# Half of the third branch's merge products issued inside the convolution stage of a hybrid Hyena, FNet, mLSTM and mixture-of-experts layer

## The chip, the cores and the metric

The kernel runs on one core of a Trainium2 chip. The metric is device microseconds of one execution on that core; lower is better. A profiled execution shows what the engines did: PE (TensorE, the matrix engine), DVE (VectorE), ACT (ScalarE), POOL (GpSimd) and SP (SyncE, which here only starts transfers). Each engine takes its instructions in order.

## The reference, cut to what matters

One layer over 1024 tokens of width 1024, all in float32. Three branches (a Hyena long convolution, a grouped FNet and a bidirectional mLSTM) each give 512 channels. The merge projects each branch to 1024 channels, weighs it by a sigmoid gate and sums:

```python
def merge_branches(y_hy, y_fn, y_ml, gate_pre, lp):
    B, L, _ = gate_pre.shape
    dt = gate_pre.dtype
    ys = jnp.stack([y_hy, y_fn, y_ml], axis=2).astype(dt)
    proj = jnp.einsum("blkc,kcd->blkd", ys, lp["w_branch"])
    g = jax.nn.sigmoid(gate_pre.astype(jnp.float32)).reshape(B, L, N_BRANCH, D_MODEL).astype(dt)
    return jnp.sum(g * proj, axis=2) @ lp["w_out"]
```

The change is in the product `ys[2] @ w_branch[2]`, the mLSTM branch `y_ml`. Nothing that is computed changes.

## The kernel before, in words

A float32 product is made of three products of a shorter type. `split` (L215, L216) writes a value's upper part (ACT, a cast) and the rest (DVE or POOL, a subtraction); `mm3` (L230 to L232) issues upper by upper, lower by upper and upper by lower into one PSUM tile. So every operand that comes from DRAM costs a transfer, a cast on ACT and a subtraction on DVE or POOL, and every product three instructions on PE.

The kernel's stages follow one another: filters, projections, mLSTM, FNet, the gate projections, the Hyena convolutions (`stage_conv`), the merge (`stage_merge`), the output projection and the experts. The mLSTM and the FNet results lie in DRAM (`yd[2]`, `yd[1]`) long before the convolutions begin. The Hyena result `yd[0]` is written when they end.

**The convolutions.** Four passes (order 0 and 1, each for two halves of 256 channels), each of eight blocks `(par, fb)`: four of the even part, four of the odd part. A block has a forward product (`conv_fwd`, tiles `gp`: 12 instructions of 256 columns for an even block, 24 for an odd one). DVE then multiplies with the filter (`kk`, L1057), sums (`t`, L1059) and splits into `yh` (ACT) and `yl` (DVE). The inverse product (`conv_inv`, tiles `acc`, 12 instructions of 256 or 512 columns) follows two blocks later. At the fifth block the next pass's input is prepared (`conv_in`): DVE folds the previous pass's output (`f`), PE transposes it (L1023, 16 instructions a pass), ACT copies it (`raw`), DVE and ACT split it (`u2`, `u1`). That input is the result of `conv_out`, a chain on DVE over the second half of the pass before. In PSUM `gp` has two banks and `acc` six, all eight.

**The merge.** A loop over the branches 2, 1, 0 and, in each, over eight blocks `d` of 128 output channels. Per `d` PE issues 24 instructions of 512 columns (two halves of the tokens, four channel tiles `k`, three products). The weights `m` come from DRAM (256 KB; cast on ACT, subtracted on POOL) and so does the gate `g` (512 KB). For the first branch DVE writes `acc = (g + 1) * p` (L1539); for the other two it multiplies in `g`, and POOL adds. The branch's four input tiles `y` (512 KB each) go through the buffers `y` of pool `GA`, two in all, so the load of the third waits until the first is split (L216 `yl`). Gates have three buffers, raw weights two, output weights `w` in pool `GT` two. During the second branch the eight tiles of `w_out` are loaded too.

**Order.** Tile's scheduler orders each engine's instructions by its own estimate of time; the program's order and the priorities are only its input. SP starts nearly all transfers, in one queue, and a transfer that waits for a buffer holds back those behind it.

## Time and profile before

| | us |
|---|---|
| runs: lowest, median, highest of 3 | 1661.92, 1670.61, 1671.79 |
| the profiled execution's own time | 1670.78 |
| its span, first to last instruction | 1669.0 |
| convolutions, from the first forward product | about 906 to 1078 |
| first branch of the merge | about 1078 to 1123 |
| second and third branch | about 1123 to 1208 |

Positions are microseconds from the start of the span. A row of the view by stretches gives the busy time of each engine in it and the number of its instructions, the clock granted to TensorE as a share of 2.4 GHz (0.5 is the lower level, 1.2 GHz), the share of the 16 DMA engines' time in use, and GB/s. A matrix instruction's own duration is longer than its place in the queue, since the next starts before it ends: what one costs is read from start to start.

### The profile page before, as it was taken

The page shows a single profiled execution, that of the slowest core. Times are in us where ns is not written, and L with a number is a line of the kernel's source. Part 1 is how long each engine was busy: PE and PEld are TensorE (multiplying, and loading weights), DVE is VectorE, ACT ScalarE, POOL GpSimd, SP SyncE. Part 2 cuts the span into 40 slices and gives each one's busy share as a digit, 9 for nine tenths or more (in the row PEclk, how much of TensorE's full clock was granted, in tenths as well). Part 3 has the DMA queues.
Part 4 walks back from the last instruction along what each step waited for, and adds up shares of the span by engine and source line. Part 5 has one row for each costly group of instructions (what it writes and reads, how often), then busy time and mean ns, then how long its engine had stood idle before and what let it go on. Part 6 is the DMA issues. An engine that isn't in the chain of part 4 may idle for free. (4 is left out here: it accounts for less than half of the span.)

```text
span 1669.0 us, 22629 instructions
## 1 busy us (share of the span) xinstructions
PE 1557.4 (93%) x8489; PEld 1307.7 (78%) x8489; DVE 1179.0 (71%) x1764; ACT 686.2 (41%) x1052; POOL 303.1 (18%) x277
## 2 busy tenths in 40 slices
PE   6999999999999999899988899999999869999992
PEld 2678877788888887778877788888888769999992
DVE  3898785966786869788644999953255567767776
ACT  3566454433222124444424443332033444544553
POOL 0000000000000001000002000127523353565641
PEclk8999999999999999999998998999999979999996
DMA  7453576422232374877424433685363388999984
GB/s 287 139 199 137 213 239 219 144 81 81 101 110 89 129 261 169 295 265 245 157 107 159 140 102 100 229 313 180 135 255 114 139 252 251 300 282 289 264 233 169
DMA packets 125570, 315.97 MB, mean 189 GB/s; under 512 B 17689, under 2 KB 43281, under 8 KB 125458
## 3 DMA queue, kind: packets, MB, share of 16 engines
q1 hardware_dynamic: 113354, 279.77, 48.6%
q0 software_dynamic: 10496, 32.36, 8.1%
q10 hardware_dynamic: 1608, 2.37, 0.4%
q8 instruction: 68, 1.11, 0.3%
q14 instruction: 44, 0.36, 0.1%
HBM read 227.53 MB, written 86.91 MB: 188 GB/s over the span
## 5 line engine op out<-in xcount | busy, mean ns | idle before, releaser
L230 PE MATMUL gp<-ht,wh 128*128 128x512 f32 x768 | 303.9, 396 | 4.6 <-ACT wh L215 3.5
L232 PE MATMUL gp<-ht,wl 128*128 128x512 f32 x768 | 302.1, 393 | 0.9 <-DVE wl L216 0.9
L231 PE MATMUL gp<-ht,wh 128*128 128x512 f32 x768 | 302.5, 394 | 0.0
L230 PEld LDWEIGHTS gp<-ht,wh 128*128 128x128 f32 x768 | 145.0, 189 | 37.7 <-ACT wh L215 4.4
L232 PEld LDWEIGHTS gp<-ht,wl 128*128 128x128 f32 x768 | 145.0, 189 | 31.1 <-DVE wl L216 1.5
L231 PEld LDWEIGHTS gp<-ht,wh 128*128 128x128 f32 x768 | 145.1, 189 | 29.0 <-issue 0.2
L230 PE MATMUL pb<-xh,gh 128*128 128x224 f32 x512 | 142.7, 279 | 0.0
L231 PE MATMUL pb<-xl,gh 128*128 128x224 f32 x512 | 141.6, 277 | 0.8 <-issue 0.8
L232 PE MATMUL pb<-xh,gl 128*128 128x224 f32 x512 | 141.7, 277 | 0.0
L801 DVE SCALAR_TENSOR_TENSOR u<-z,hy_cw,u 128x945 f32<-128x945 f32 (+2 forms) x96 | 117.3, 1222 | 13.3 <-ACT u L793 11.1
L216 DVE TENSOR_TENSOR wl<-w,wh 128x1024 fp32r<-128x1024 f32 x57 | 70.4, 1236 | 58.5 <-ACT wh L215 58.1
L215 ACT CAST wh<-w 128x1024 fp32r<-128x1024 f32 x57 | 59.8, 1051 | 122.1 <-PE gp L231 83.4
L232 PEld LDWEIGHTS pb<-xh,gl 128*128 128x128 f32 x512 | 99.4, 194 | 0.8 <-issue 0.8
L230 PEld LDWEIGHTS pb<-xh,gh 128*128 128x128 f32 x512 | 99.3, 194 | 0.3 <-ACT xh L215 0.2
L231 PEld LDWEIGHTS pb<-xl,gh 128*128 128x128 f32 x512 | 99.4, 194 | 0.1
L801 DVE SCALAR_TENSOR_TENSOR u<-z,ml_cw,u 128x945 f32<-128x945 f32 (+2 forms) x64 | 77.9, 1220 | 27.4 <-ACT u L793 26.4
L786 ACT ACTIVATE z<-gp,b_cols 128x512 f32<-128x512 f32 x46 | 31.4, 684 | 136.8 <-PE gp L232 136.8
L216 POOL TENSOR_TENSOR ml<-m,mh 128x512 fp32r<-128x512 f32 x24 | 35.2, 1468 | 208.8 <-ACT mh L215 208.8
L949 POOL MEMSET z<- 128x1024 f32 x1 | 1.0, 961 | 359.1 <-DVE u L801 359.1
L786 ACT ACTIVATE z<-gp,bh 128x512 f32<-128x512 f32 x46 | 31.4, 684 | 76.4 <-PE gp L232 56.6
L1806 DVE TENSOR_TENSOR gl<-x,gh 128x1024 fp32r<-128x1024 f32 x33 | 40.5, 1233 | 29.1 <-ACT gh L1804 21.6
L1778 POOL DMA_INDIRECT sum<-y,sidx x26 | 45.4, 1744 | 79.5 <-DVE y L1887 75.9
(618 smaller groups left out, 3986.9 us busy)
## 6 DMA issues: line engine op xcount, KB each, us to landing
w<-in_ada_rest SPq DMA_DIRECT2D x32, 512.0 KB
w<-in_w_gu SPq DMA_DIRECT2D x32, 512.0 KB
x<-in_w_gu SPq DMA_DIRECT2D x32, 512.0 KB
w<-in_w_gate SPq DMA_DIRECT2D x24, 512.0 KB
g<-gd SPq DMA_DIRECT2D x24, 512.0 KB
gd<-z SPq DMA_DIRECT2D x23, 512.0 KB
r<-in_ada_in SPq DMA_DIRECT2D x16, 512.0 KB
pd<-ft SPq DMA_DIRECT2D x32, 256.0 KB
```

Of the source, the lines that this page charges most:

```text
L215: self.copied = nc.scalar.copy(hi, src)
L216: return (nc.vector if eng == "v" else nc.gpsimd).tensor_sub(lo, src, hi.bitcast(F32))
L230: mm(ps, lh, rh, start=start, stop=False)
L231: mm(ps, lh, rl, start=False, stop=False)
L232: mm(ps, ll, rh, start=False, stop=stop)
L786: return lambda s, p: self.nc.scalar.activation(z[:, s], p, func, bias=bias, scale=scale)
L801: last = nc.vector.scalar_tensor_tensor(ui[:, r0:r1, c0:c1], zi[:, r0 + dy:r1 + dy, c0 + dx:c1 + dx], taps[:, i:i + 1], ui[:, r0:r1, c0:c1 ...
L949: nc.gpsimd.memset(zt, 0.0)
L1778: return self.nc.gpsimd.indirect_dma_start(out=out, out_offset=bass.IndirectOffsetOnAxis(ap=ix, axis=0), in_=src, in_offset=None, **kw)
L1806: lo = (nc.vector if engines[i] == "v" else nc.gpsimd).tensor_sub(ml, m, mh.bitcast(F32))
```

## The change

A generator `branch_first` computes the first 512 tokens of the mLSTM branch's product inside the convolutions: it loads the first half of the four tiles `yd[2]` (256 KB each, four casts, four subtractions on DVE) at block 4 of the first pass. Then, for each of the eight `d`, it loads and splits the weights (now also on DVE) and issues twelve instructions of 512 columns in four steps of three, into a PSUM tile `fl`. ACT copies the sum into `z`, SP writes it to DRAM (`bd`). A step stands behind the forward product of each block from block 6 of the first pass on, and a second one in the blocks 2 and 6 of a pass. For `fl` one bank is taken from `acc`, which has five now. Pool `CF` holds the new tiles.

In the merge's first branch only the second 512 tokens are multiplied (12 instructions per `d` in place of 24), `y` tiles are loaded by halves, and each `bd[d]` (256 KB) is loaded through the two buffers `w` of pool `GT`. DVE's multiplication is in two halves, one from `bd` and one from PSUM. Weights and gates of that branch are loaded as before. The number of PE's instructions is the same.

```diff
--- before.py
+++ after.py
@@ -188,7 +188,7 @@
         self.n += 1
         return self.dp.tile(list(shape), dt, name=f"{name}_{self.n}", tag=f"{name}_{self.n}")
 
-    PSB = {"gp": 2, "q": 2, "b1": 2, "pb": 1, "acc": 6, "ph": 8}
+    PSB = {"gp": 2, "q": 2, "b1": 2, "pb": 1, "acc": 5, "fl": 1, "ph": 8}
 
     def ps(self, tag="pb", shape=(128, 1024)):
         self.n += 1
@@ -1141,10 +1141,32 @@
         for kind in "fi":
             self.mat(kind, 0, 0, 0)
 
+    def branch_first(self):
+
+        nc = self.nc
+        self.bd = self.dram([8, 128, 512], name="bd")
+        ys = [self.parts("CF", "y", 4, self.load("CA", "ms", 4, self.yd[2, ct, :, :512], (128, 512))) for ct in range(4)]
+        weights = lambda d: self.parts("CF", "w", 2, self.load("CA", "ms", 4, self.A["w_br"][2, d], (128, 4, 128)))
+        ws = [weights(0)]
+        yield
+        for d in range(8):
+            mh, ml = ws.pop()
+            p = self.ps("fl", (128, 512))
+            for k in range(4):
+                self.mm3(p, mh[:, k, :], ml[:, k, :], *ys[k], k == 0, k == 3)
+                if k == 1 and d < 7:
+                    ws.append(weights(d + 1))
+                if k == 3:
+                    z = self.t("CF", "z", 2, F32, (128, 512))
+                    nc.scalar.copy(z, p)
+                    nc.sync.dma_start(self.bd[d], z)
+                yield
+
     def stage_conv(self):
         nc = self.nc
         self.pool("C1")
         self.pool("CN")
+        self.pool("CF")
         self.psum("conv")
         blocks = [(par, fb) for par in range(2) for fb in range(4)]
         passes = [(o, half) for o in range(2) for half in range(2)]
@@ -1152,6 +1174,7 @@
         for fb in (1, 2, 3):
             self.mat("f", 0, 0, fb)
         first = self.copied, self.lower
+        fill = self.branch_first()
         with self.tc.issue_after(self.copied.ins):
             for f in self.rest:
                 f()
@@ -1168,6 +1191,12 @@
                     for i in () if n or j else first:
                         es.enter_context(self.tc.issue_after(i.ins))
                     y = self.conv_fwd(ut[n], o, half, par, fb)
+                if (n, j) == (0, 4):
+                    next(fill)
+                if (n, j) > (0, 5):
+                    next(fill, None)
+                    if j % 4 == 2:
+                        next(fill, None)
                 if len(last) == 2:
                     self.conv_inv(*last.pop(0))
                 if j == 1 and n:
@@ -1181,7 +1210,10 @@
             self.conv_inv(*a)
         for _ in self.conv_out(acc[3], 1, 1):
             pass
+        for _ in fill:
+            pass
         self.psum("merge")
+        self.close("CF")
         self.close("CN")
         self.close("C1")
         self.close("CT")
@@ -1520,10 +1552,13 @@
         self.wo = []
         for n, br in enumerate((2, 1, 0)):
             yh, yl = [], []
+            f = 512 if n == 0 else 0
             with self.tc.high_priority() if n == 0 else ExitStack():
                 for ct in range(4):
                     pool, tag, bufs = ("GY", "y", 4) if n == 1 else ("GN" if ct < 2 else "G", f"y{ct}", 1)
-                    h, l = self.parts(pool, tag, bufs, self.load("GA", "y", 2, self.yd[br, ct]))
+                    y = self.load("GA", "y", 2, self.yd[br, ct, :, f:], (128, L - f))
+                    h, l = (self.t(pool, tag + x, bufs, F32R)[:, f:] for x in "hl")
+                    self.split(h, l, y)
                     yh.append(h), yl.append(l)
             for d in range(8):
                 mh, ml = self.parts("GA", "m", 3, self.load("GA", "m", 2, A["w_br"][br, d], (128, 4, 128)), "g")
@@ -1531,12 +1566,14 @@
                 nc.sync.dma_start(g, self.gd[br, d])
                 p = self.ps("pb")
                 acc = self.acc[d // 4][:, d % 4, :]
-                for a in (0, 512):
+                for a in (0, 512)[n == 0:]:
                     for k in range(4):
-                        self.mm3(p[:, a:a + 512], mh[:, k, :], ml[:, k, :], yh[k][:, a:a + 512], yl[k][:, a:a + 512],
-                                 k == 0, k == 3)
+                        s = slice(a - f, a - f + 512)
+                        self.mm3(p[:, a:a + 512], mh[:, k, :], ml[:, k, :], yh[k][:, s], yl[k][:, s], k == 0, k == 3)
                 if n == 0:
-                    nc.vector.scalar_tensor_tensor(acc, g, 1.0, p, op0=ALU.add, op1=ALU.mult)
+                    b = self.load("GT", "w", 2, self.bd[d], (128, 512))
+                    nc.vector.scalar_tensor_tensor(acc[:, :f], g[:, :f], 1.0, b, op0=ALU.add, op1=ALU.mult)
+                    nc.vector.scalar_tensor_tensor(acc[:, f:], g[:, f:], 1.0, p[:, f:], op0=ALU.add, op1=ALU.mult)
                 else:
                     nc.vector.scalar_tensor_tensor(g, g, 1.0, p, op0=ALU.add, op1=ALU.mult)
                     (nc.vector if n == 2 and d > 5 else nc.gpsimd).tensor_add(acc, acc, g)
```

The scheduler's order on PE, a block of the second pass (`gp` forward, `acc` inverse, `fl` the moved products). Before:

```order
L230 MATMUL gp_7530<-u2h_7321,nh_6985 128x256
L231 MATMUL gp_7530<-u2l_7322,nh_6985 128x256
L232 MATMUL gp_7530<-u2h_7321,nl_6986 128x256
L230 MATMUL acc_7429<-mh_7149,yh_7477 128x512
L231 MATMUL acc_7429<-ml_7150,yh_7477 128x512
```

The same place of the change:

```order
L232 MATMUL gp_7586<-u2h_7355,nl_6989 128x256
L230 MATMUL fl_7610<-yh_7253,wh_7472 128x512
L231 MATMUL fl_7610<-yl_7254,wh_7472 128x512
L232 MATMUL fl_7610<-yh_7253,wl_7473 128x512
L230 MATMUL acc_7476<-mh_7152,yh_7524 128x512
L231 MATMUL acc_7476<-ml_7153,yh_7524 128x512
```

One step of three products stands between the forward and the inverse product of the block.

DVE at the end of the first pass's even blocks (`u1l` is the odd blocks' input, `f` the folds for the next pass's input, `yl` of `ms` the mLSTM tiles, `wl` the weights). Before:

```order
L216 TENSOR_TENSOR u1l_7204<-raw_6802,u1h_7203 128x512
L216 TENSOR_TENSOR u1l_7208<-raw_6828,u1h_7207 128x512
L1013 TENSOR_TENSOR f_7261<-u_7259 128x256
L1014 TENSOR_TENSOR f_7261<-u_7259 128x256
L1013 TENSOR_TENSOR f_7261<-u_7259 128x256
```

The same place of the change:

```order
L216 TENSOR_TENSOR u1l_7211<-raw_6828,u1h_7210 128x512
L216 TENSOR_TENSOR yl_7254<-ms_7251,yh_7253 128x512
L216 TENSOR_TENSOR yl_7260<-ms_7257,yh_7259 128x512
L216 TENSOR_TENSOR yl_7266<-ms_7263,yh_7265 128x512
L216 TENSOR_TENSOR yl_7272<-ms_7269,yh_7271 128x512
L1057 TENSOR_TENSOR kk_7215<-kk_7215,gp_7214 128x1024
L1013 TENSOR_TENSOR f_7295<-u_7293 128x256
L1059 TENSOR_TENSOR t_7244<-kk_7215 128x512
L216 TENSOR_TENSOR wl_7278<-ms_7275,wh_7277 128x512
L1014 TENSOR_TENSOR f_7295<-u_7293 128x256
```

Five subtractions of 512 columns now stand before or among the folds.

SP in the merge's first branch (`g` gates, `m` weights, `w` of `bd` the new halves, `y` the second branch's inputs). Before:

```order
L1531 DMA g_8995<-gd_1518 128x1024
L220 DMA y_9193<-yd_1403 128x1024
L220 DMA y_9199<-yd_1403 128x1024
L220 DMA w_9252<-in_w_out 128x1024
L1531 DMA g_9029<-gd_1518 128x1024
L220 DMA m_9091<-in_w_br 128x512
L220 DMA w_9293<-in_w_out 128x1024
L1531 DMA g_9063<-gd_1518 128x1024
L220 DMA m_9125<-in_w_br 128x512
L220 DMA y_9205<-yd_1403 128x1024
L220 DMA y_9211<-yd_1403 128x1024
```

The end of that branch in the change:

```order
L1566 DMA g_9307<-gd_1518 128x1024
L220 DMA w_9322<-bd_7250 128x512
L220 DMA y_9332<-yd_1403 128x1024
L220 DMA y_9338<-yd_1403 128x1024
L220 DMA m_9350<-in_w_br 128x512
L1566 DMA g_9356<-gd_1518 128x1024
L220 DMA w_9385<-in_w_out 128x1024
L220 DMA y_9344<-yd_1403 128x1024
```

Before, all four inputs of the second branch were started among the gates of the fourth to sixth `d` or earlier (`g_8995` is the third gate). Now three of them stand behind the eighth gate and the eighth half `w_9322`, the last one also behind a gate and a weight of the second branch.

## Rows read from the trace of the kernel before

**Rows 1.** The page's first part: busy us, share of the span, instructions

```profile
PE 1557.4 (93%) x8489; PEld 1307.7 (78%) x8489; DVE 1179.0 (71%) x1764; ACT 686.2 (41%) x1052; POOL 303.1 (18%) x277
```

**Rows 2.** Stretches: us, then PE, PEld, DVE, ACT, POOL busy, clock, DMA share, GB/s

```profile
906.00:1078.00 172.00, 155.43 (x1009) 140.86 (x1008) 157.59 (x232) 74.83 (x143) 10.34 (x7) 0.94 0.45 147
1078.00:1123.00 45.00, 44.23 (x195) 36.22 (x195) 29.08 (x29) 15.10 (x18) 11.78 (x7) 1.00 0.81 287
1123.00:1208.00 85.00, 85.00 (x377) 70.38 (x376) 27.82 (x23) 14.40 (x20) 54.09 (x48) 1.00 0.49 167
906.00:935.00 29.00, 22.06 (x135) 18.89 (x134) 24.30 (x34) 15.06 (x29) 6.07 (x4) 0.88 0.54 173
935.00:978.00 43.00, 39.43 (x264) 35.89 (x263) 39.92 (x62) 17.91 (x37) 0.00 (x0) 0.96 0.34 108
978.00:1021.00 43.00, 39.44 (x256) 36.16 (x255) 39.66 (x61) 17.43 (x35) 0.00 (x0) 0.89 0.29 95
1021.00:1078.00 57.00, 54.49 (x359) 49.93 (x359) 53.72 (x78) 24.43 (x46) 4.27 (x3) 0.99 0.59 202
```

**Rows 3.** PE's timeline: start, duration; 9 and 45 products from row to row

```profile
907.23 0.28 PE L230 MATMUL gp<-u2h,mh 128*128 128x256 f32 x1
...
908.31 0.28 PE L230 MATMUL gp<-u2h,nh 128*128 128x256 f32 x1
...
1115.64 0.39 PE L231 MATMUL pb<-y1l,mh 128*128 128x512 f32 x1
...
1125.84 0.39 PE L231 MATMUL pb<-yl,mh 128*128 128x512 f32 x1
```

**Rows 4.** What PE waited for, 900 to 1080: us, times, longest

```profile
PE acc L230 <- ACT yh L215: 6.8, 6, 1.8
PE gp L1023 <- DVE f L1007: 2.3, 1, 2.3
...
PE gp L230 <- ACT raw L1026: 0.2, 1, 0.2
```

**Rows 5.** Four shorter stretches, columns as in rows 2

```profile
970.00:980.00 10.00, 6.50 (x33) 5.09 (x34) 7.03 (x12) 4.53 (x10) 0.00 (x0) 0.83 0.21 58
1010.00:1020.00 10.00, 8.28 (x39) 7.31 (x40) 7.61 (x12) 1.76 (x5) 0.00 (x0) 0.58 0.14 45
1050.00:1060.00 10.00, 8.18 (x67) 7.77 (x66) 10.00 (x11) 3.82 (x6) 2.98 (x2) 1.00 0.86 279
1090.00:1100.00 10.00, 10.00 (x45) 8.26 (x44) 7.66 (x6) 4.56 (x7) 3.12 (x2) 1.00 0.91 344
```

**Rows 6.** DVE's groups by line, 906 to 1078: busy us, mean ns, idle before

```profile
L216 DVE TENSOR_TENSOR yl<-t,yh 128x512 fp32r<-128x512 f32 x32 | 21.6, 686 | 1.6 <-ACT yh L215 1.3
...
L216 DVE TENSOR_TENSOR y0l<-y,y0h 128x1024 fp32r<-128x1024 f32 x1 | 1.2, 1227 | 0.0
```

**Rows 7.** DVE's timeline at the end of two passes

```profile
926.74 1.89 DVE L216 TENSOR_TENSOR u1l<-raw,u1h 128x512 fp32r<-128x512 f32 x3
928.54 0.42 DVE L1013 TENSOR_TENSOR f<-u 128x256 f32<-128x256 f32 x1
...
977.63 0.69 DVE L1030 TENSOR_TENSOR t<-raw,raw 128x512 f32<-128x512 f32 x1 [2.79 <-ACT raw L1026]
```

**Rows 8.** The merge's first product on PE, its first multiplication on DVE

```profile
1078.29 0.39 PE L230 MATMUL pb<-y0h,mh 128*128 128x512 f32 x1
...
1086.37 1.21 DVE L1539 SCALAR_TENSOR_TENSOR acc<-g,pb 128x1024 f32<-128x1024 f32 x1
```

**Rows 9.** SP starts two loads of y and one; ACT casts them on landing

```profile
1094.65 1.46 SPq L220 DMA_DIRECT2D y<-yd  x2
...
1127.58 0.33 SPq L220 DMA_DIRECT2D y<-yd  x1
...
1101.21 1.06 ACT L215 CAST yh<-y 128x1024 fp32r<-128x1024 f32 x1 [0.22 <-DMA y<-yd]
...
1130.94 1.05 ACT L215 CAST y2h<-y 128x1024 fp32r<-128x1024 f32 x1 [2.41 <-DMA y<-yd]
```
## The prediction

> **What bounds the kernel now.** I read the page's first part, then the busy times by stretches, then PE's timeline, its waits and the short stretches where it waits, then DVE, and last the transfers of the merge. PE is busy for 93% of the span and DVE for 71% [rows 1]. That is the mean over unlike stages, so the stages must be read apart [rows 2]. In the merge (1078 to 1208) PE is busy throughout at a granted clock of 1.00, while DVE works 29 of 45 us and 28 of 85: there the end is set by PE's number of instructions. In the convolutions (906 to 1078) both engines are nearly full: PE 155.4 and DVE 157.6 of 172 us. The change takes work from a stage where PE alone decides into one where PE has some room and DVE hardly any.
>
> What a product takes in PE's queue is read from start to start [rows 3]: nine products of 256 columns in 1.08 us give 0.12 us each, 45 of 512 columns in 10.20 us give 0.227 us. By the code the convolutions have, in four passes, 768 products of 256 columns (4 x (4 x 12 + 4 x 24 + 4 x 12)) and 192 of 512: 92.2 + 43.6 us. Three sets of 16 transposes, priced at no more than 0.12 us, add 5.8. PE's bare work is 141.6 of 172 us; 30.4 are left. Where are they? Nine kinds of wait, from 6.8 us for ACT's `yh` down to 0.2, add to 16.4 us [rows 4]. The granted clock of 0.94 means that 0.06 x 172 = 10.3 us of full-rate time are missing [rows 2]; short stretches at 0.83 and 0.58 hold most of that, and PE waits in them [rows 5]. So the room is real, but it lies where one pass hands over to the next (970, 1010, 1050) and in the first 29 us, not everywhere.
>
> **What the change takes out of the merge.** 96 products of 512 columns: 96 x 0.227 = 21.8 us. PE is the bound there [rows 2], so this is a full gain unless something else is late.
>
> **What it adds to the convolutions.** The same 21.8 us on PE, which makes 163.4 us of bare work. On DVE twelve subtractions of 512 columns (four `y`, eight weights; those weights were POOL's work in the merge). One lasts 0.69 us [rows 6] and takes 0.60 from start to start: three take 1.8 [rows 7]. That is 7.2 us; two half-size splits for the merge in place of two of 1.2 us give back 1.2. DVE comes to 163.6 us. On ACT twelve casts and eight copies of 0.5 to 0.7 us lie beside 97 us of its idle time [rows 2]. The added transfers, some 5 MB, fall where the DMA share is 0.14 to 0.54 [rows 2, 5].
>
> Both engines would then have about 163.5 us of work in a stage of 172, and they feed each other block by block. From below the growth is nothing, if every step falls into a wait. From above all is exposed: 21.8 + 6.0 = 27.8 us. I work it out by stretches. In the first (906 to 935) five subtractions now stand before or among DVE's folds, for which PE's transposes wait: 5 x 0.6 = 3 us; the first block of twelve products lies inside that wait and costs nothing more. The next two passes take about ten steps each, 6.8 us of PE. In such a pass PE has 3.6 us without any work and 0.04 to 0.11 x 43 = 1.7 to 4.7 us of missing clock [rows 2]; but only two to four products of a step stand at the handover itself, the rest between blocks where PE and DVE are both unbroken. I let 4 us of the 6.8 be absorbed and 2.8 exposed, plus nothing for DVE. The last pass has nine steps (6.1 us) and 2.5 us of idle PE in its 57 us: 3.6 exposed. Sum: 3 + 2.8 + 2.8 + 3.6 = 12.2; fuller PE should lose less clock, for which I give back 2. I take 10 us. The accumulators have five banks for six, so three in place of two of four tiles of the odd blocks wait for an eviction; no row prices it. One DVE instruction (0.6 us) at each of seven such turns, 4 us, bounds it from above, nothing from below; I leave it inside the 10.
>
> **What becomes late in the merge.** The first branch now takes 8 x 12 x 0.227 = 21.8 us on PE. Before, it had 44, in which the second branch's inputs were loaded early. Now three of those inputs stand on SP behind the last gate and the last half `bd`, whose two buffers come free as DVE multiplies. DVE's first multiplication started 8.1 us after the first product [rows 8]; with smaller splits before it, 7. A load takes from 3.4 us (alone, from 1127.58 to the cast at 1130.94) to some 5.8 (the second of a pair, started about 1095.4, cast at 1101.21) [rows 9]. Each two `d` cost one load, an issue of 0.4 and a multiplication of 0.7. From the first product on, with 3.4: the sixth `d` is multiplied at 18, inputs two and three start at 19, the second is split behind DVE's last multiplication at 24, and only that frees the buffer for the fourth: start 24.7, landing 28.1, cast (1.05) and subtraction (1.13) until 30.3. PE wants it after 21.8 + 9 x 0.227 = 23.8. It is 6.5 us late, and three products of the next `d` fit in: 5.8. With 5.8 for every load the same chain ends at 40, 15 us late. The nearest row is between: the DMA engines are at 0.91 in 1090 to 1100 [rows 5], but half of these loads are of 256 KB. I take 7.5 us, with a slower clock after the wait in it. From below the price is nothing, should the loads be as early as PE needs them. The rest of the merge keeps its length: eight `w_out` tiles move from the first into the second branch, where 85 us are at 0.49 [rows 2].
>
> **Sum.** -21.8 + 10 + 7.5 = -4.3 us against the profiled execution's own 1670.8 (span 1669.0 and 1.8 around it), which is the median of the runs (1670.6): 1666.5 us.
>
> **Rivals.**
> A: the fillers hold the clock. For it: PE fell to 0.58 of full rate at 1010 to 1020, next to waits [rows 5], and the 10.3 us of missing clock are a third of PE's room. Were no clock lost, the convolutions would grow by the 3 us at the first handover alone: -21.8 + 3 + 7.5 = -11.3, 1659.5 us; with the late inputs at nothing as well, 1652. Against it: DVE would have 163.6 us of work and its own waits, such as 2.8 us for ACT's copies [rows 7]. The Trainium skill says in "TensorE: Matmul & The Clock Gate", section "What's actually happening", that the throttled rate is the default and that activity releases it. By that rule A is the outcome; the trace agrees so far that the low rate stands next to waits.
> B: the steps lengthen the loop from PE over DVE and ACT to PE. In order, each step keeps the inverse product behind it waiting, its accumulator is evicted later, and DVE, full already, gets its next operand later. If all 32 steps and the splits are exposed the stage grows by 27.8: -21.8 + 27.8 + 7.5 = +13.5, 1684.3 us. It is slower than before once the growth passes 14.3 us. For it: DVE at 157.6 of 172 [rows 2]. Against it: PE's 16.4 us of waits [rows 4].
> C: the late inputs decide. Each load takes 5.8 us: -21.8 + 10 + 15 = +3.2, 1674 us. For it: 344 GB/s at a share of 0.91 before the branch was shortened [rows 5].
>
> **How the numbers follow.** The forecast has 0.55, with a range of its own of 1662 to 1672; A 0.24, B 0.11, C 0.10. A difference of 1% (16.7 us) is about what a measurement of this kernel can tell from no change. Faster by more needs nearly all of A and no late inputs: half of A and a little of the forecast's edge, 0.13. Slower by more needs more than B's whole price: half of B and a little of C, 0.06. The rest, 0.81, is within 1%. The range reaches from the better half of A to below B's end: 1655 to 1680.
>
> **What would show it.** Right: the stretch from the first forward product to the merge's first is about 182 us (172 before); its granted clock is above 0.94; the merge's first branch takes PE some 22 us and is followed by a wait of 6 to 9 us on ACT's or DVE's split of `y`; from there to the merge's end it is 85 us as before. A is right if the stretch is 175 us or less at a clock near 1.00, B if it is over 186 with PE's waits for `yh` and DVE's for `gp` grown, C if the wait at the second branch is over 12 us with the transfer as its releaser. The prediction is wrong if the convolutions do not grow, or if the second branch starts at once.

## The result and the profile after

The changed kernel is slower by half a per cent: 1675.82 us (median of 18 runs, 1669.16 to 1679.58) against 1667.43 us (18 runs, 1661.21 to 1671.79), a ratio of 1.0056 with a 95% interval of 1.0045 to 1.0068, some 9 us. The forecast was 1666.5 us in a range of 1655 to 1680: the time lies in the range, the direction was wrong. The profiled execution of the changed kernel took 1676.74 us with a span of 1675.0, 6.0 us longer than the span before.

The page's first part is nearly that of [rows 1], so the totals tell nothing: the same products are done elsewhere.

```profile
PE 1558.5 (93%) x8489; PEld 1305.8 (78%) x8489; DVE 1183.9 (71%) x1784; ACT 696.4 (42%) x1072; POOL 309.0 (18%) x277
```

The stretches of the changed kernel, cut at the same points as [rows 2] (us, then PE, PEld, DVE, ACT, POOL busy, clock, DMA share, GB/s): the convolutions whole, their four passes, the merge's first branch, its other two.

```profile
906.00:1089.00 183.00, 172.78 (x1111) 155.40 (x1110) 161.28 (x244) 85.05 (x163) 10.85 (x7) 0.97 0.50 160
906.00:940.00 34.00, 25.66 (x153) 21.33 (x151) 27.41 (x40) 19.57 (x36) 6.44 (x4) 0.90 0.74 236
940.00:982.00 42.00, 42.00 (x288) 38.35 (x286) 41.20 (x64) 20.22 (x40) 0.00 (x0) 1.00 0.38 121
982.00:1026.00 44.00, 43.91 (x289) 39.69 (x288) 41.39 (x65) 19.91 (x39) 0.00 (x0) 1.00 0.41 124
1026.00:1089.00 63.00, 61.21 (x387) 56.04 (x387) 51.29 (x78) 25.35 (x50) 4.42 (x3) 0.97 0.52 170
1089.00:1121.00 32.00, 25.60 (x100) 19.93 (x99) 20.19 (x28) 7.30 (x10) 7.88 (x6) 0.89 0.83 307
1121.00:1219.00 98.00, 92.09 (x385) 73.32 (x385) 39.63 (x33) 22.79 (x29) 61.47 (x50) 0.97 0.57 202
```

Two things differ. In the second and third pass PE now has no idle time and a clock of 1.00 (before: 3.6 us idle each, clock 0.96 and 0.89). In the merge, where PE had been busy throughout at 1.00, it now idles 6.4 and 5.9 us and loses clock.

The exact cuts are five products in PE's timeline of the changed kernel (start, duration): the first into an accumulator of the convolutions, the first of each branch of the merge, the merge's last.

```profile
913.90 0.39 PE L230 MATMUL acc<-mh,yh 128*128 128x256 f32 x1 [1.26 <-ACT yh L215]
...
1089.35 0.39 PE L230 MATMUL pb<-y0h,mh 128*128 128x512 f32 x1
...
1120.83 0.39 PE L230 MATMUL pb<-yh,mh 128*128 128x512 f32 x1
...
1173.36 0.39 PE L230 MATMUL pb<-y0h,mh 128*128 128x512 f32 x1
...
1218.70 0.39 PE L232 MATMUL pb<-y3h,ml 128*128 128x512 f32 x1
```

In the kernel before the same five start at 912.44, 1078.29, 1122.89, 1166.41 and 1209.71. So the parts last:

| part | before, us | after, us | difference | forecast |
|---|---|---|---|---|
| convolutions | 165.85 | 175.45 | +9.6 | +10 |
| merge, first branch | 44.60 | 31.48 | -13.1 | -21.8 |
| second branch | 43.52 | 52.53 | +9.0 | +7.5 |
| third branch | 43.30 | 45.34 | +2.0 | 0 |
| sum | 297.27 | 304.80 | +7.5 | -4.3 |

The rest of the span (1.5 us more ahead of the first point, 3.0 less behind the last) is in no part that the change touches. The convolutions came out as forecast in their sum, and 96 products did leave the merge. The loss is data that comes late, in all three branches: 8.7 + 9.0 + 2.0 = 19.7 us, where 7.5 was allowed.

**What PE waits for in the merge.** The waits of PE in the changed kernel, 1080 to 1215 (us in total, times, longest):

```profile
PE pb L230 <- ACT mh L215: 6.3, 1, 6.3
PE pb L230 <- ACT yh L215: 2.9, 1, 2.9
PE pb L232 <- POOL ml L216: 0.9, 2, 0.7
PE pb L231 <- DVE y3l L216: 0.8, 1, 0.8
PE pb L231 <- DVE yl L216: 0.7, 2, 0.5
PE pb L230 <- ACT y3h L215: 0.6, 1, 0.6
```

The largest is not for an input `yh`, which the prediction had counted, but for a weight `mh`, which it had not: the seventh of the first branch. Waits alone are 12.2 us. Most of the rest of the 19.7 is the clock behind the two largest, as PE's timeline at that wait shows (start, duration, then the idle time before and its releaser):

```profile
1105.58 0.39 PE L232 MATMUL pb<-y3h,ml 128*128 128x512 f32 x1
1112.24 0.79 PE L230 MATMUL pb<-y0h,mh 128*128 128x512 f32 x1 [6.28 <-ACT mh L215]
...
1117.17 0.63 PE L231 MATMUL pb<-y3l,mh 128*128 128x512 f32 x1
```

After the wait a product of 512 columns lasts 0.63 us and not 0.39. The stretches behind these two waits show the lower of the two levels, 1.2 in place of 2.4 GHz:

```profile
1112.00:1117.00 5.00, 4.63 (x10) 3.23 (x11) 0.69 (x1) 0.81 (x2) 2.54 (x2) 0.50 1.02 391
...
1128.00:1135.00 7.00, 6.29 (x15) 4.31 (x15) 2.12 (x2) 2.32 (x4) 3.58 (x2) 0.52 0.87 330
```

**Why the weight is late.** ACT's timeline: the cast of that weight had waited for its transfer, and ACT had been idle for 10.89 us.

```profile
1099.64 1.05 ACT L215 CAST yh<-y 128x1024 fp32r<-128x1024 f32 x1
1111.57 0.62 ACT L215 CAST mh<-m 128x512 fp32r<-128x512 f32 x1 [10.89 <-DMA m<-in_w_br]
```

SP's timeline shows where the load stood. SP starts its DMAs in order: `m` raw weights, `w<-bd` stored halves (two buffers), `g` gates (three buffers, line 1566), `y` inputs. Between the weights at 1094.48 and the next at 1107.30 stand an input, four stored halves and three gates. DVE's timeline gives the reason up to 1099.27: its first multiplication (line 1575), the one that gives a half and a gate their buffers back, starts only at 1098.56, behind the closing multiplications of the convolutions (line 1126). From there on the two buffers go in a circle: a half has to land before DVE can multiply it (it waits 2.20 us for the one started at 1099.27) and so free the buffer for the next, and SP stands again until 1104.56.

```profile
1085.59 0.80 SPq L1566 DMA_DIRECT2D g<-gd  x1
1094.48 0.33 SPq L220 DMA_DIRECT2D m<-in_w_br  x1
1094.91 0.38 SPq L220 DMA_DIRECT2D y<-yd  x1
1099.27 0.32 SPq L220 DMA_DIRECT2D w<-bd  x1
...
1104.56 0.32 SPq L220 DMA_DIRECT2D w<-bd  x1
1104.93 0.42 SPq L1566 DMA_DIRECT2D g<-gd  x1
1106.89 0.32 SPq L220 DMA_DIRECT2D w<-bd  x1
1107.30 0.38 SPq L220 DMA_DIRECT2D m<-in_w_br  x1
```

```profile
1096.24 2.39 DVE L1126 TENSOR_TENSOR f<-u,f 128x512 f32<-128x512 f32 x2
1098.56 0.68 DVE L1575 SCALAR_TENSOR_TENSOR acc<-g,w 128x512 f32<-128x512 f32 x1
...
1103.84 0.69 DVE L1575 SCALAR_TENSOR_TENSOR acc<-g,w 128x512 f32<-128x512 f32 x1 [2.20 <-DMA w<-bd]
```

The raw weights have two buffers, which POOL gives back when it has split them. Its timeline shows the split that ended at 1094.45, just ahead of the load at 1094.48, and the next, which ended at 1098.09: the late load had its buffer 9.2 us before SP came to it.

```profile
1092.92 1.53 POOL L216 TENSOR_TENSOR ml<-m,mh 128x512 fp32r<-128x512 f32 x1 [18.48 <-ACT mh L215]
1096.79 1.30 POOL L216 TENSOR_TENSOR ml<-m,mh 128x512 fp32r<-128x512 f32 x1 [2.33 <-ACT mh L215]
```

### The profile page after: what moved, and what is told of

It is laid out like the page before. It is cut to its first block, busy times and chain, and to the rows that moved or that the text cites. A ratio compares the mean times of both kernels' runs of the same rounds, so it can differ in the third digit from the quotient of the medians.

```text
span 1675.0 us, 22724 instructions
## 1 busy us (share of the span) xinstructions
PE 1558.5 (93%) x8489; PEld 1305.8 (78%) x8489; DVE 1183.9 (71%) x1784; ACT 696.4 (42%) x1072; POOL 309.0 (18%) x277
```

## The experiments

Three theories of the late data were tested. **Q, the queue:** loads of weights stand on SP behind loads that wait for buffers. **V, the volume:** the same bytes must now come in less time, whatever their order. **D, DVE:** its late start holds everything back. In the names of waits and tiles `m` is always a raw weight of the merge, `g` a gate, `bd` the stored halves. Columns of the table: convolutions, and the first two branches of the merge together (their products alone are 65.4 us where half of the first is gone, 24 x 12 products of 0.227; 76.3 in the runs with four added products), both by the cuts above and from one profiled execution each; then the ratio to the kernel before with its interval.

| run | convolutions, us | two branches, us | ratio (95%) |
|---|---|---|---|
| before | 165.85 | 88.12 | 1 |
| changed kernel | 175.45 | 84.01 | 1.0056 (1.0045 to 1.0068) |
| e1_own | 174.99 | 78.86 | 1.0036 (1.0020 to 1.0051) |
| e5_bdact | 175.07 | 78.93 | 1.0077 (1.0056 to 1.0098) |
| e8_inplace | 174.12 | 82.15 | 1.0039 (1.0025 to 1.0053) |
| e9_both | 177.58 | 78.57 | 1.0031 (1.0015 to 1.0047) |
| e10_halfg | 173.93 | 78.30 | 1.0056 (1.0035 to 1.0076) |
| e11_mpool | 175.35 | 76.15 | 0.9977 (0.9962 to 0.9992) |
| e17_mypoolhp | 176.43 | 79.02 | 1.0005 (0.9988 to 1.0022) |
| e18_all | 178.71 | 78.77 | 1.0014 (0.9997 to 1.0032) |
| e20_mhp | 175.76 | 80.03 | 0.9995 (0.9981 to 1.0009) |
| e24_beforem | 163.83 | 88.14 | 0.9997 (0.9979 to 1.0015) |
| e3_convonly | 176.23 | 88.14 | 1.0068 (1.0046 to 1.0091) |
| e4_mergeonly | 164.78 | 82.39 | 0.9941 (0.9920 to 0.9961) |
| e2_acc5 | 164.03 | 88.14 | 1.0013 (0.9997 to 1.0030) |
| e6_poolsplit | 172.80 | 84.32 | 1.0069 (1.0045 to 1.0093) |
| e21_quarter | 173.40 | 77.43 | 0.9972 (0.9956 to 0.9987) |
| e22_quartersp | 169.83 | 77.25 | 0.9974 (0.9959 to 0.9990) |

A ratio is worth more than a profile here: ten runs with the changed kernel's code for the convolutions (its own and e3_convonly among them) took 173.9 to 177.6 us for it in their one profile each. A profiled execution can also lie off its run's median: e10_halfg's (1671.37 us, median 1679.39) and e11_mpool's (1662.93, median 1667.35) below it, e4_mergeonly's (1664.44, median 1661.19) and e22_quartersp's (1668.99, median 1664.96) above. The edits below are cut to the lines that matter.

### Buffers in place of waits: e1_own, e8_inplace, e9_both, e5_bdact

```diff
 # e1_own
-b = self.load("GT", "w", 2, self.bd[d], (128, 512))
+b = spare[d][:, :f].bitcast(F32)    # spare: the first branch's eight input tiles
+nc.sync.dma_start(b, self.bd[d])
 # e8_inplace, second branch
+y = l.bitcast(F32)
+nc.sync.dma_start(y, self.yd[br, ct])
 # e5_bdact
+nc.scalar.dma_start(b, self.bd[d])
```

> The changed kernel, with a place of its own for each of the eight stored halves (the unused first half of the first branch's input tiles) in place of two rotating buffers. Theory Q (the issue queue): the raw weights of the first branch come late because their loads stand on SP behind loads of stored halves that wait for a buffer which DVE's multiplications free. Then the 6.3 us wait for the seventh weights' part goes, and with it the half-clock products behind it (about 2.7 us); the loads of the second branch's inputs are still behind, so its 2.9 us wait may stay. Expected 1664 to 1669 us on the scale where the changed kernel stands at 1675.8, a ratio to the kernel before of 0.997 to 1.002. Rival V (volume): the transfers of this stretch (304 GB/s, DMA busy 0.83) can't come sooner in any order; the wait stays within 2 us and the time within 3 us of the changed kernel's. Rival D (DVE): the first branch's multiplications start 9 us after its first product and hold everything; then the wait for the weights goes, but PE waits as long for the free accumulator, and the time stays within 3 us.

> The changed kernel with the second branch's four inputs loaded straight into the tiles that later hold their lower parts, split there in place, so that their loads wait for no raw buffer. Theory Q: the wait for the fourth input at the second branch's start (2.9 us, with about 3.6 us of half clock behind it) needs the raw buffer's wait as well as the queue; this goes or shrinks to under 1 us, 3 to 7 us below the changed kernel; the 6.3 us wait for the seventh weights stays or grows, since these loads now may stand ahead of it. Rival V: moving loads about gains nothing, within 3 us. Rival D: the second branch starts when DVE has freed the accumulator, within 3 us.

> Both edits: stored halves each in a place of its own, and the second branch's inputs loaded in place. Theory Q: both waits go; the merge's three branches then cost the kernel before's less 21.8 us of products, plus what is left of late data (under 4 us): 12 to 16 us below the changed kernel, a ratio to the kernel before of 0.995 to 0.999, faster than both. Rival V: no gain over the changed kernel beyond 3 us, since the same bytes must come in the same 30 us. Rival D: under 5 us, with PE waiting for DVE.

> The changed kernel with the loads of the stored halves issued from ACT's queue in place of SP's; their two buffers and their waits stay. Theory Q: SP no longer stands behind the buffer, weights and inputs are issued earlier, and the waits for the seventh weights (6.3 us) and the fourth input (2.9 us) shrink; but ACT now stands in the same wait and casts later, so a part may come back as a wait for ACT. Expected 3 to 10 us below the changed kernel if ACT's standing costs little, and no gain with PE waiting for ACT's casts if it costs as much. Rival V: within 3 us of the changed kernel, with the same PE waits for late data. Rival D: within 3 us.

Measured: 1.0036, 1.0039, 1.0031 and 1.0077. Each of the first two gives back about 3 us (0.0020 and 0.0017 of the time, little more than the intervals can tell from nothing), both together 4, and moving the same wait to ACT's queue nothing (there the third branch grew to 51.2 us). In e1_own the longest wait for `mh` shrank from 6.3 to 2.8 us and did not go. Theory Q had said 7 to 12 us for e1_own and 12 to 16 for e9_both: as I had put it, it fell. SP's timeline of e9_both shows why. With the halves out of the way the weights stand behind the gates, whose buffers DVE frees too: four gates hold SP for 7.02 us.

```profile
1100.19 0.33 SPq L220 DMA_DIRECT2D m<-in_w_br  x1
1101.93 7.02 SPq L1573 DMA_DIRECT2D g<-gd  x4
1109.04 0.39 SPq L220 DMA_DIRECT2D m<-in_w_br  x1
```

The queue was not excluded, only the stored halves as the one load that blocks it. The next runs take the weights off the queue, or take bytes away.

### The weights on a queue of their own, and fewer bytes: e11_mpool, e10_halfg

```diff
 # e11_mpool
-mh, ml = self.parts("GA", "m", 3, self.load("GA", "m", 2, A["w_br"][br, d], (128, 4, 128)), "g")
+m = self.t("GA", "m", 2, F32, (128, 4, 128))
+nc.gpsimd.dma_start(m, A["w_br"][br, d])
+mh, ml = self.parts("GA", "m", 3, m, "g")
 # e10_halfg
-nc.sync.dma_start(g, self.gd[br, d])
+nc.sync.dma_start(g[:, f:], self.gd[br, d, :, f:])
-nc.vector.scalar_tensor_tensor(acc[:, :f], g[:, :f], 1.0, b, op0=ALU.add, op1=ALU.mult)
+nc.vector.scalar_tensor_tensor(acc[:, :f], g[:, f:], 1.0, b, op0=ALU.add, op1=ALU.mult)
```

> The changed kernel with the raw weights of the merge issued from POOL's queue, which frees their buffers itself, in place of SP's, where they stand behind gates and stored halves. Theory Q: the 6.3 us wait for the seventh weights' part goes, and about 2.7 us of half clock with it, 5 to 9 us below the changed kernel, unless POOL's later work holds the queue. Theory V: the weights come early, but the gates and inputs come as much later, and PE waits for the accumulators or the fourth input instead: within 3 us of the changed kernel.

> The changed kernel with half of each gate of the first branch loaded (256 KB in place of 512 KB, eight times: 2 MB less), the second half standing in for the first, so the gates of that branch's first half are left out; buffers, queue and multiplications stay. Theory V (the bytes of the merge's start): in the 20 us from 1099 the DMA engines are 0.93 to 0.99 busy at 324 to 370 GB/s, so 2 MB less is about 6 us earlier data: 5 to 8 us below the changed kernel. Theory Q (SP stands behind buffers that DVE frees): the buffers come free at the same times, the waits stay within 2 us of the changed kernel's, and the time within 3 us.

e11_mpool: 0.9977, which is 0.79% or 13 us under the changed kernel, more than Q had asked for, and under the kernel before. The 6.3 us wait is gone and the first branch lasts 23.4 us, close to its products. Its waits in the merge, 1065 to 1215, and its two branches as stretches:

```profile
PE pb L230 <- ACT mh L215: 2.7, 3, 1.4
PE pb L232 <- POOL ml L216: 1.7, 3, 0.8
...
PE pb L230 <- ACT yh L215: 0.7, 1, 0.7
```

```profile
1089.00:1113.00 24.00, 23.18 (x100) 18.22 (x100) 20.45 (x26) 5.30 (x8) 12.93 (x11) 1.00 0.80 292
1113.00:1166.00 53.00, 48.32 (x195) 37.54 (x194) 33.99 (x25) 20.22 (x23) 30.79 (x23) 0.94 0.79 288
```

The second branch is still 9 us longer than its products: that part of the late data is left. Its fourth input lands no earlier than in the changed kernel, 36.9 us after the merge's first product (1089.95) against 37.3 there; ACT's casts of it, in the changed kernel and in e11_mpool:

```profile
1126.60 1.04 ACT L215 CAST yh<-y 128x1024 fp32r<-128x1024 f32 x1 [3.73 <-DMA y<-yd]
```

```profile
1126.85 1.05 ACT L215 CAST yh<-y 128x1024 fp32r<-128x1024 f32 x1 [0.88 <-DMA y<-yd]
```

e10_halfg brings 2 MB less and gains nothing by its ratio (1.0056), where V had said 5 to 8 us; in its one profile the two branches do gain 5.7 us and the third gives 4.6 back (49.9 us, waiting for its own inputs). So taking bytes away alone gave no time back, and V alone does not explain the loss. That the bytes play no part is not shown. For POOL's queue the Trainium skill says in "DMA: Bandwidth & Descriptors", section "Issuing engines are not separate DMA queues", that starting DMAs from several engines saves only the time that issuing takes. Here the issue is 0.3 to 0.4 us a load and the gain 13 us, so the measurement goes beyond that: SP's rows show a queue that works in order and stands behind a buffer, and the weights no longer wait for it.

### Further along that way: e17_mypoolhp, e18_all, e20_mhp

```diff
 # e17_mypoolhp: e11_mpool, and the second branch's inputs in place from POOL's queue, ahead
-with self.tc.high_priority() if n == 0 else ExitStack():
+with self.tc.high_priority() if n <= 1 else ExitStack():
+nc.gpsimd.dma_start(y, self.yd[br, ct])
 # e18_all: e11_mpool, inputs on POOL's queue without priority, and
-z = self.t("CF", "z", 2, F32, (128, 512))
+z = self.load("CF", "z", 2, self.gd[2, d, :, :512], (128, 512))   # the gate's half
-nc.scalar.copy(z, p)
+nc.vector.scalar_tensor_tensor(z, z, 1.0, p, op0=ALU.add, op1=ALU.mult)
-nc.vector.scalar_tensor_tensor(acc[:, :f], g[:, :f], 1.0, b, op0=ALU.add, op1=ALU.mult)
+nc.sync.dma_start(acc[:, :f], self.bd[d])
 # e20_mhp: e11_mpool, and around the first branch's two multiplications
+with self.tc.high_priority():
```

> The changed kernel with the raw weights on POOL's queue, as in the run before, and with the second branch's inputs loaded in place and from POOL's queue too, ahead of the first branch's later work. Theory Q: the rest of the late data at the second branch's start (some 3 us of waits and the half clock behind them, its first branch 23.4 us and second branch 52.8 us where 22 and 44 are the products alone) shrinks: 2 to 8 us below the run with the weights alone, 1659 to 1666 us. Theory V: the inputs (2 MB) take the gates' and weights' place in the 20 us where the DMA engines are full, and PE waits in the first branch instead: within 2 us of that run, or above it.

> The same without the priority, and with the first half's gates applied in the convolutions: DVE multiplies each added product by its gate while storing it, in place of ACT's copy, and the merge loads the finished half straight into its accumulator, so that eight multiplications of 0.69 us and 2 MB of gates leave the merge and no buffer of the stored halves is left to wait for. By Q and V alike the merge's waits shrink: 5 to 12 us below the changed kernel with the weights alone on POOL's queue if the merge was all that was lost, 1655 to 1663 us; if DVE's eight operations or the eight gate loads lengthen the convolutions, 0 to 5 us of that come back.

> The changed kernel with the weights on POOL's queue, and the first branch's multiplications ahead of DVE's other work where the scheduler can: the first four move ahead of the last pair of the convolutions' closing multiplications (2.39 us). Theory D: DVE's late start sets when gates' and halves' buffers come free, and the half clock and waits left in the second branch (52.8 us where 44 are its products) come from it: 2 to 5 us below the run with the weights alone. Rival (the transfers are what is late from 1109 on, at 355 to 367 GB/s): within 2 us of that run.

None gains on e11_mpool: 1.0005, 1.0014, 0.9995. In e18_all POOL's timeline shows the weights once more behind loads that wait, now the inputs `yl` on the same queue; the two weights at 1118.68 come after them, and PE waits 7.3 us for `mh`:

```profile
1110.45 0.57 POOL L1569 DMA_DIRECT2D m<-in_w_br  x1
1111.02 1.07 POOL L1564 DMA_DIRECT2D yl<-yd  x2
1116.90 1.27 POOL L216 TENSOR_TENSOR ml<-m,mh 128x512 fp32r<-128x512 f32 x1 [4.81 <-ACT mh L215]
1118.12 0.56 POOL L1564 DMA_DIRECT2D yl<-yd  x1
1118.68 1.09 POOL L1569 DMA_DIRECT2D m<-in_w_br  x2
```

e18_all also takes DVE's eight multiplications and 2 MB out of the merge, and its first two branches still last 78.8 us; since its weights stand behind the inputs, it separates neither V nor D from Q. e20_mhp puts the first four multiplications ahead of 2.39 us of DVE's closing work, so that the first starts 5.7 us after the merge's first product in place of 9.6 in e11_mpool, and gains nothing. D was not supported by that shift; a larger one wasn't tried.

### Is it the change that made the queue matter? e24_beforem

The same edit as e11_mpool, in the kernel before.

> The kernel before with the merge's raw weights on POOL's queue, the one edit that made the changed kernel faster. Theory Q: in the kernel before the weights never came late (no PE wait for them in the merge), so the queue gains nothing there: within 3 us of the kernel before, 0.998 to 1.002, and the gain in the changed kernel is the wait that the change had made. Rival (the queue is better for any merge): 4 to 9 us below the kernel before.

Measured 0.9997, no difference, as Q had it: with 44 us of products in the first branch the weights come in time from either queue.

### The two halves of the change apart: e3_convonly, e4_mergeonly

```diff
 # e3_convonly: the merge whole, the stored halves unused
-f = 512 if n == 0 else 0
+f = 0
-for a in (0, 512)[n == 0:]:
+for a in (0, 512):
 # e4_mergeonly: no added products
-fill = self.branch_first()
-b = self.load("GT", "w", 2, self.bd[d], (128, 512))
+b = self.load("GT", "w", 2, self.yd[2, d % 4, :, :512], (128, 512))
```

> The changed kernel's convolutions, with their added products, over the kernel before's merge: the merge computes both halves of the third branch itself, so the added products are done twice and their stored results are not read. By the two profiles the convolutions cost 9.6 us more and the rest nothing: 1676 to 1679 us on the scale where the kernel before stands at 1667.4, a ratio of 1.005 to 1.007. Rival (what follows pays too): the later start of the merge changes what comes after it; then the ratio lies outside 1.003 to 1.009.

> The kernel before's convolutions (no added products, six accumulators) with the changed kernel's merge; the first half of the third branch's product is left out, and a load of the same size of other stored data stands in its place. By the two profiles the merge gains 13.1 us in the first branch and gives back 11.1 us in the other two: 1663 to 1667 us, a ratio of 0.997 to 1.000. If the 21.8 us of removed products came through with only the 7.5 us of late inputs that the prediction allowed, the ratio is 0.990 to 0.993.

e3_convonly: 1.0068, 11 us, in the expected range; its merge is the kernel before's (44.6 + 43.5 us), so a merge that only starts later loses nothing. e4_mergeonly: 0.9941, a gain of 10 us where 0 to 5 was expected, a miss. Its profile shows only half of that in the merge, which lasts 126.4 us against 129.4 in the changed kernel and 131.4 before: 82.4 us for the two branches, with the weights late as in the changed kernel, and 44.0 for the third. The two ratios add to 1.5 us, the changed kernel shows 9; the difference is more than the two intervals (3.4 and 3.8 us to either side) leave room for, and what the halves do to each other stays open.

### What the convolutions pay: e2_acc5, e6_poolsplit

```diff
 # e2_acc5, in the kernel before
-PSB = {"gp": 2, "q": 2, "b1": 2, "pb": 1, "acc": 6, "ph": 8}
+PSB = {"gp": 2, "q": 2, "b1": 2, "pb": 1, "acc": 5, "ph": 8}
 # e6_poolsplit: the added products' splits on POOL
-self.parts("CF", "w", 2, ...)
+self.parts("CF", "w", 2, ..., "g")   # and the same for the inputs "y"
```

> The kernel before with five accumulators of the convolutions in place of six, and nothing else. The added products cost the convolutions 9.6 us by the two profiles, of which they carry 21.8 us of PE work; this asks how much of the 9.6 is the lost accumulator. Theory F (the added products themselves, with what they bring to DVE and ACT): 0 to 2 us above the kernel before, a ratio of 0.999 to 1.002. Rival (the sixth accumulator): PE waits at the handovers for DVE's reading of the one accumulator fewer, 5 to 10 us, a ratio of 1.003 to 1.006.

> The changed kernel with the lower parts of the added products' inputs and weights made on POOL, which is almost idle in the convolutions, in place of DVE. If DVE's share of the added work (twelve splits of 0.69 us, 8.3 us) is what the convolutions pay, 3 to 8 us below the changed kernel; if it is the products on PE, within 2 us; if POOL's longer operation (1.3 to 1.8 us) makes the weights late, slower.

e2_acc5: 1.0013, an interval that holds 1; the sixth accumulator is worth 5 us at most and its profile shows the convolutions no longer (164.0 us). Whether it costs more beside the added products is not tested. e6_poolsplit: 1.0069, no gain from a freer DVE. What the convolutions pay is then, by exclusion, the products on PE. The stretches agree: of the 21.8 us, PE's idle time gives back 6.4 (16.6 before, 10.2 after) and the clock about 5 (0.94 of 172 us, 0.97 of 183), which leaves about the 11 us by which the stretch grew. The middle passes had that room; the last pass had 2.5 us of idle time and grew by 6.

### Half as many added products: e21_quarter, e22_quartersp

```diff
-for d in range(8):          # the products that go into the convolutions
+for d in range(4):
-if (n, j) > (0, 5):
+if (n, j) > (0, 5) and j % 2 == 0:
-    if j % 4 == 2:
+    if j == 2:
-for a in (0, 512)[n == 0:]:
+half = n == 0 and d < 4
+for a in (0, 512)[half:]:
```

> The changed kernel with the weights on POOL's queue, and only the first four of the eight added products in the convolutions, a step behind every second block; the other four are whole in the merge. The convolutions get 10.9 us of PE work in place of 21.8, the merge 33 us of products in its first branch in place of 22, in which the same bytes must come. If the convolutions hide added work evenly (12 of 21.8 us), they cost 5 us over the kernel before; if the first half hides better, 0 to 3 us. The merge then needs no late data: first branch 33 us, second 44, third 44. Expected 1657 to 1663 us, under both kernels; if the waits in the merge stay (over 6 us), 1664 to 1669.

> The same with the weights on SP's queue, as in the changed kernel. Theory Q: four stored halves still stand on SP ahead of the later weights, but the products are longer by 11 us, so most of the wait is covered: 2 to 6 us above the run before it. Theory V: the bytes have 11 us more to come in and the queue matters little: within 2 us of that run.

0.9972 and 0.9974: both beat both kernels, the kernel before by 0.3%, and the queue makes no difference any more (for e22_quartersp Q had asked for 2 to 6 us, so V's expectation held there). In the waits of e21_quarter, 1060 to 1215, nothing of the merge's first two branches is left (the `acc` row is the convolutions' end, `y2l` the third branch's, as in the kernel before), and the stretches show PE full at a clock of 1.00:

```profile
PE acc L230 <- ACT yh L215: 3.1, 2, 2.6
PE pb L231 <- DVE y2l L216: 0.8, 1, 0.8
```

```profile
1085.00:1120.00 35.00, 34.23 (x151) 27.72 (x150) 27.12 (x30) 11.30 (x14) 14.61 (x13) 1.00 0.81 291
1120.00:1163.00 43.00, 43.00 (x191) 35.63 (x190) 27.43 (x19) 14.88 (x18) 30.84 (x22) 1.00 0.68 243
```

With all eight products moved, no order of the loads brought the merge's first two branches below 76 us, although PE needs 65.4; with four moved they take 77.3, 1 us more than PE's own 76.3. The second half of the products that left the merge bought at most 1.3 us there (e11_mpool), in the other orders nothing, and cost the convolutions 2 to 6 us by these profiles (175.4 against 173.4 and 169.8; 165.9 before). The first half thus cost 4 to 8 us, where 0 to 5 had been expected; since profiles of the same code differ by almost 4 us, that it cost half of the 10 is not shown. e11_mpool and e21_quarter are equal within their intervals.

What sets the 76 us is open. In e11_mpool the DMA engines are 0.79 to 0.80 busy on the mean of the two branches, but not evenly: SP stands from 1091.85 to 1100.24 until DVE frees a half's buffer, with the engines at 0.43 from 1094 to 1100, and then they are full while PE waits:

```profile
1114.00:1120.00 6.00, 2.62 (x6) 0.98 (x5) 2.58 (x4) 1.61 (x3) 3.22 (x3) 0.87 1.02 386
1120.00:1126.00 6.00, 5.74 (x15) 4.36 (x16) 2.45 (x2) 2.76 (x3) 0.76 (x2) 0.56 0.96 348
```

So the late start of the transfers and their bytes can both be behind it, and no run separates the two. In e21_quarter the engines are as full from 1099 to 1129 (0.98 to 1.00), and PE, with more products to do, does not wait.

## Why the prediction was wrong, point by point

- **"What the change takes out of the merge", -21.8 us:** right as far as the products go; e11_mpool's first branch (23.4 us) shows the price. The condition "unless something else is late" was the whole question.
- **"What it adds to the convolutions", +10 us:** 9.6 by the profiles, 11 by e3_convonly. Its parts were less good. The middle passes (42 and 44 us for 43 and 43) took the steps almost free, where 2.8 us each had been charged, because the clock rose to 1.00 and PE's gaps closed; the first (34 for 29, of it 1.5 a later start) and the last (63 for 57) paid more than 3 and 3.6. That the sum still came out at 10 is in part luck: these errors cancel. The bound of 4 us for the lost accumulator is not contradicted (2 us by e2_acc5, 5 at most).
- **"What becomes late in the merge", +7.5 us: the step that failed.** It followed only the second branch's inputs on SP and did not ask about the weights. They stood on the same queue behind the same halves and gates, and were later than the inputs: 6.3 us of wait inside the first branch, 2.9 for the fourth input. With the clock behind these two waits and the third branch's own late inputs it came to 19.7 us. e11_mpool, which moves only the weights, gives 13 us back; e24_beforem shows that the same move is worth nothing where the branch is long. The term that was followed was too small as well: the fourth input landed 37.3 us after the first product and not 28.1. PE waited only 2.9 us for it because the weights had already held PE back; with the weights on time (36.9 us, e11_mpool) the second branch still lasts 9 us longer than its products.
- **DVE's first multiplication** was put at 7 us after the first product (8.1 before, [rows 8]); it came at 9.2 (1098.56 - 1089.35). The chain that was built on it started 2 us late.
- **The clock** was charged in the convolutions but not in the merge, beyond "a slower clock after the wait" within the 7.5. Two stretches of 5 and 7 us at 0.50 and 0.52 cost some 2.5 and 3.4 us, half their length.
- **Rivals.** A was half right: the fillers held the clock in two passes, but the convolutions still grew. B did not happen: DVE's 161.3 us of work are below the 163.6 expected, freeing it gained nothing, and PE's waits for `yh` in the convolutions fell from 6.8 to 5.1 us. C was nearest in its time (1674 us) and in its place, the data. Its chain also comes out in its end, though not in every link: with 5.8 us a load the fourth input lands at about 38 us, and 37.3 was measured (the second took 6.1 us, from 1111.28 to its cast at 1117.40; the fourth, alone, 3.7, but it started 33.5 us after the first product, where the forecast had 24.7). What it lacked is the weights: its sign, a wait of over 12 us at the second branch, did not appear, since the largest wait came before.
- **The signs named beforehand:** 182 us from the first forward product to the merge was right (181.5, from 907.87 to 1089.35), the clock above 0.94 too (0.97); a first branch of 22 us followed by one wait was wrong, the wait came inside it; 85 us for the rest was wrong (98).

## What to carry to other kernels

When work is taken out of a stage that the compute engine bounds, list every load that must land in the shortened time, in the order of the queue that issues it, and ask of each which buffer it waits for; a load that is never late today can be the latest tomorrow because of the one ahead of it. Taking out as much as the data can follow and no more (here half) gave the same time as the best order of loads found for all of it. A wait of a few microseconds on the tensor engine should be priced with the half clock that can follow it, as it did here behind the two largest.

## What the runs showed of the hardware

- After PE's waits of 6.28 and 2.92 us the granted clock was 0.50 to 0.52 for the next 5 to 7 us, though PE had work for nearly all of it; with 2.5 and 3.4 us of lost clock the waits cost 1.4 and 2.2 times their own length.
- Issuing a DMA takes 0.56 us on POOL, against 0.3 to 0.4 us on SP; POOL was still the better place for the changed kernel's weights by 13 us.
- With the DMA engines at 1.02 of their time an input of 512 KB, the first of two, took 5.6 us from its start to its cast (e11_mpool, 1114.00 to 1119.62), against 3.4 us for one alone in the kernel before.
